# First sweep: gate products copied from PSUM by VectorE, the gate's last multiplication from the copy on GpSimd

## The chip, the core and the metric

The kernel runs on one core of a Trainium2 chip. The metric is the device time of one execution in microseconds; the median of three runs before the change was 1300.88 us (1297.87 to 1301.57). The engines are TensorE (PE in the profile; PEld is its loading of weights), VectorE (DVE), ScalarE (ACT), GpSimd (POOL) and SyncE (SP, which here only issues DMAs). Each engine works through its own queue in order, and waits on semaphores for the others.

## The reference

One layer of an encoder over 2048 positions of width 1024. A combined projection `x @ w_in` feeds two groups of heads. Group A is a gated linear attention with a forward and a backward scan in chunks; its output is normalised per head and multiplied with a SiLU gate. Group B is a latent attention with a dense softmax, gated in the same way. Both halves go through one output projection, and a layer norm of `alpha * x + mixer(x)` ends the layer. The change concerns group A's gate alone:

```python
    o = rms_norm(o_fwd + o_bwd, norm_g)
    o = o.reshape(B, S, D_GLA).astype(gate.dtype)
    return o * jax.nn.silu(gate)
```

## The kernel before

All products are made in float32 from a high and a low part of each operand, three matmuls for one product (`mm3`, L417 to L421). A high part is a rounding copy on ACT (`hi`, L362 to L367), a low part the subtraction of the high part from the original, on DVE or POOL (`lo`, L369 to L371). L365 and L371 therefore stand for many different operations in the profile, which are told apart by the tiles they write.

The kernel has four stages: a first sweep over 16 chunks of 128 positions, from chunk 15 down to chunk 0 (`sweep_a`), the late gates and the weights of the next stage (`late_gates`), a second sweep over the chunks upwards (`sweep_c`), and the softmax attention with the output projection (`attention`, `OutProj`).

For a chunk the first sweep makes three groups of products (`ipa`, 288, 384 and 384 columns), then the 512 columns of the gate (`ipg`, `gate_products`). These four results take turns in the two PSUM banks of the pool `ip`: the second group of the next chunk comes into the bank in which the gate's products lay. Between them stand the operations of the chunk before: transposes of q and k (`qT`, `kT`, L937 and L961), the decayed `qd` (L941) and `kd` (L965), their splitting (`qbh`, `qbl`, `kh`, `kl`), the transposed keys (`kt`, L979), the products `Ap`, `Up` and `Op`. The gate's decay comes from the low-rank part `lr` of the first group: `lr` is split on ACT and DVE (`ga_lr`), transposed by PE (`lrT`, L869), copied by ACT (`lrTs`), and multiplied by PE into `z` (L881). From `z` come, over three ACT steps and DVE's `za` (L891), the scans L902 and L904, and from those `E` (L914) and its two exponentials (L918, L920), which `qd` and `kd` need. `cw` (L927) are the decays of the state.

POOL makes the low part of the next but one chunk's input (`xal`, L371; on DVE for the first chunks), and the update of the running state (`Us` L1042, `Sb` L1048 and L1067, `Sm` L1063).

The gate itself is `silu` (L1485 to L1496): three ACT steps, an exponential, a logarithm and an exponential, make the sigmoid in an SBUF tile `gs` or `ub`; DVE then multiplies it with the products, which it reads from PSUM. Fourteen gates, those of chunks 13 to 0, run in the sweep (`ga_gs`, L839, in the first steps; `gate_end`, L829, in the others and for chunk 0) with tag `gs`; those of chunks 15 and 14 come behind it, with tag `ub`. Each result is stored to `u_s` (L833 or L846), and the second sweep reads it (`c_lu`). The stores of chunks 0 and 1 are issued by POOL, all others by SP.

In the first steps (chunks 14 to 12) the order of the work on every engine is written out by hand (`ORDER_A`). From chunk 11 on a scheduler sets it, from the program's order, the places in `STEPS_A` and its own estimate of when each operation is ready. It also puts operations of different engines that use the same PSUM bank one behind the other. The second sweep starts with chunk 0; its loads from `oi_s`, `qd_s` and `su_s` (L1381) stand in SP's queue with the loads of small weights (L1153). Its POOL operations `Sf` (L1399, L1402) and `SU` (L1407) make the state from `su_s`, which is split into `MMb`, and PE multiplies it into `Ob` (L1430, L1431).

Of the kernel before, what the change touches and what calls it, by code (L numbers as in the profile page):

```python
# [9 lines left out]
F32 = mybir.dt.float32  # L10
# [3 lines left out]
ALU = mybir.AluOpType  # L14
# [340 lines left out]
class K:  # L355
# [1129 lines left out]
    def silu(self, pool, g, shape, tag, name):  # L1485

        nc = self.nc
        t = self.sl = pool.tile(shape, F32, tag=tag, name=f"{tag}{name}", bufs=3 if tag == "ub" else 1)
        nc.scalar.activation(t, g, AF.Exp, scale=-1.0)
        yield 0  # L1490
        nc.scalar.activation(t, t, AF.Ln, bias=1.0)
        yield 1
        nc.scalar.activation(t, t, AF.Exp, scale=-1.0)
        yield 2
        nc.vector.tensor_tensor(t, g, t, ALU.mult)
        yield 3  # L1496


# [525 lines left out]
```

## Time and profile before

| | |
|---|---|
| median of 3 runs | 1300.88 us (1297.87 to 1301.57) |
| profiled execution | 1303.84 us, its span 1301.6 us |
| granted TensorE clock over the span | 0.996 |
| first sweep, repeating part, 95 to 342 us | 247 us; DMA share 0.25 |
| late gates and start of the second sweep, 342 to 366 us | 24 us; PE busy 22.98, DMA share 0.90 |
| second sweep, 366 to 640 us | 274 us; PE busy 269.60, POOL 157.80 |
| attention, 640 to 1245 us | 605 us; PE busy 598.61 |
| end, 1245 to 1302 us | 57 us; PE busy 48.43 |

A row of the profile's groups names the line, the engine, the operation, the tile written and those read, the shape and the count; behind the bar stand the busy time in us and the mean time of one in ns, and then the time for which the engine stood idle before them and what ended it. A row of the timeline has the start in us, the duration, and the instruction (xN: that many in a row), with an idle time of the engine before it in brackets. A row of the waits names who waited for whom, the total in us, how often, and the longest.

### The profile page before, as it was taken

How to read it: one execution, taken by the hardware profiler on the slowest of the kernel's cores; microseconds unless marked ns; L12 is line 12 of the kernel's file. 1: busy time of each engine (PE TensorE's matmuls, PEld its weight loads, DVE VectorE, ACT ScalarE, POOL GpSimd, SP SyncE). 2: the span in 40 equal slices, each digit the busy share in tenths (PEclk: the TensorE clock that was granted, in tenths of full speed). 3: DMA queues.
4: the chain of work that ended last, by engine and by line, in shares of the span. 5: the costliest groups of instructions: out<-in, count | busy, mean ns of one | idle time of the engine just before them, and what ended most of it. 6: DMA issues, size and time to landing. Idle time of an engine off the chain costs nothing.

```text
span 1301.6 us, 19963 instructions
## 1 busy us (share of the span) xinstructions
PE 1273.0 (98%) x7017; PEld 1122.8 (86%) x7017; DVE 927.6 (71%) x1712; ACT 817.4 (63%) x1387; POOL 785.4 (60%) x500
## 2 busy tenths in 40 slices
PE   7999999999999999999999999999999999998997
PEld 7999999999889999999788888888888888886886
DVE  6865664545665555555888888888888888386998
ACT  7765556565676566555788887888888887411110
POOL 0244232332567666661398888889999999934441
PEclk9999999999999999999999999999999999999999
DMA  8232222131566555656301112212233110376563
GB/s 288 72 90 66 81 66 81 53 94 53 200 203 192 187 179 200 206 179 203 96 1 41 42 41 50 52 46 57 57 89 90 41 41 25 121 241 163 189 203 102
DMA packets 113964, 145.82 MB, mean 112 GB/s; under 512 B 18018, under 2 KB 70630, under 8 KB 113864
## 3 DMA queue, kind: packets, MB, share of 16 engines
q1 hardware_dynamic: 105176, 142.41, 35.6%
q0 software_dynamic: 768, 2.10, 0.4%
q8 instruction: 56, 0.92, 0.3%
q10 hardware_dynamic: 7920, 0.03, 0.3%
q14 instruction: 44, 0.36, 0.1%
HBM read 94.14 MB, written 50.36 MB: 111 GB/s over the span
## 4 chain that ended last, share of the span: by engine, by line
PE 83%; DMA 4%; DVE 3%; ACT 3%; POOL 2%; issue 2%; SPq 0%; DVEq 0%; POOLq 0%; ACTq 0%
PE o L419 4%; PE o L420 4%; PE pS L1533 4%; PE o L421 4%; PE pS L1535 4%; PE pS L1536 4%; PE pS L1537 4%; PE pS L1534 4%; PE ipa L419 4%; PE ipa L421 3%; PE ipa L420 3%; PE pz L420 2%; PE pz L419 2%; PE pz L421 2%; PE ipg L419 2%; PE ipg L420 2%
## 5 line engine op out<-in xcount | busy, mean ns | idle before, releaser
L371 POOL TENSOR_TENSOR pl<-s,ph 128x1024 fp32r<-128x1024 f32 x128 | 306.4, 2413 | 58.4 <-ACT ph L365 54.6
L1555 DVE TENSOR_TENSOR rm<-pS,rm 128x512 f32<-128x512 f32 x210 | 144.9, 690 | 36.6 <-ACT s L1542 31.5
L1542 ACT ACTIVATE s<-pS 128x1024 f32<-128x1024 f32 x128 | 131.5, 1027 | 60.8 <-PE pS L1537 52.3
L1579 DVE TENSOR_TENSOR s<-s,mb 128x1024 f32<-128x1024 f32 x128 | 151.2, 1213 | 9.1 <-PE mb L1573 9.0
L1042 POOL TENSOR_TENSOR Us<-Us,cw 128x512 f32<-128x512 f32 x16 | 18.6, 1162 | 212.4 <-DVE Us L1040 180.7
L365 ACT ACTIVATE ph<-s 128x1024 fp32r<-128x1024 f32 x128 | 135.1, 1057 | 17.1 <-PE o L421 16.6
L1583 ACT ACTIVATE s<-s 128x1024 f32<-128x1024 f32 x128 | 131.4, 1050 | 13.4 <-DVE s L1579 13.3
L419 PE MATMUL ipa<-wah,xah 128*128 128x384 f32 (+1 forms) x384 | 131.2, 342 | 6.9 <-ACT wah L365 6.4
L420 PE MATMUL ipa<-wal,xah 128*128 128x384 f32 (+1 forms) x384 | 125.5, 327 | 0.1
L421 PE MATMUL ipa<-wah,xal 128*128 128x384 f32 (+1 forms) x384 | 124.8, 325 | 0.0
L1533 PE MATMUL pS<-qh,ckvT_h 128*128 128x512 f32 x256 | 102.5, 400 | 0.8 <-ACT s L1583 0.4
L419 PE MATMUL o<-ph,vh 128*128 128x512 f32 x256 | 101.0, 395 | 0.0
L421 PE MATMUL o<-ph,vl 128*128 128x512 f32 x256 | 99.8, 390 | 0.0
L1536 PE MATMUL pS<-rh,krs 128*128 128x512 f32 x256 | 99.8, 390 | 0.0
L1535 PE MATMUL pS<-qh,ckvT_l 128*128 128x512 f32 x256 | 99.8, 390 | 0.0
L1537 PE MATMUL pS<-rl,krs 128*128 128x512 f32 x256 | 99.7, 389 | 0.0
L1534 PE MATMUL pS<-ql,ckvT_h 128*128 128x512 f32 x256 | 99.7, 389 | 0.0
L420 PE MATMUL o<-pl,vh 128*128 128x512 f32 x256 | 99.7, 389 | 0.0
L371 POOL TENSOR_TENSOR ol<-of,oh 128x512 fp32r<-128x512 f32 x32 | 42.9, 1343 | 70.4 <-ACT oh L365 69.6
L1606 DVE TENSOR_TENSOR ap<-ap,s 128x512 f32<-128x512 f32 x120 | 83.1, 692 | 2.6 <-ACT s L1583 0.7
L419 PEld LDWEIGHTS ipa<-wah,xah 128*128 128x128 f32 x384 | 72.9, 190 | 9.9 <-ACT wah L365 6.6
L419 PE MATMUL pz<-xch,wzh 128*128 128x256 f32 x256 | 74.8, 292 | 0.0
(325 smaller groups left out, 3825.2 us busy)
## 6 DMA issues: line engine op xcount, KB each, us to landing
xcf<-xT_dram SPq DMA_DIRECT2D x16, 512.0 KB, 4.5
xr<-x_dram SPq DMA_DIRECT2D x16, 512.0 KB, 5.7
out_dram<-rr SPq DMA_DIRECT2D x32, 256.0 KB, 2.4
xaf<-xT_dram SPq DMA_DIRECT2D x14, 512.0 KB, 3.8
oib<-oi_s SPq DMA_DIRECT2D x16, 256.0 KB, 3.9
qdb<-qd_s SPq DMA_DIRECT2D x16, 256.0 KB, 5.0
SU<-su_s SPq DMA_DIRECT2D x16, 256.0 KB, 4.4
ub<-u_s SPq DMA_DIRECT2D x16, 256.0 KB, 4.2
```

What stands on the lines that cost most here:

```text
L365: return nc.scalar.activation(dst, src, AF.Copy).ins
L371: return e.tensor_tensor(dst, src, hi.bitcast(F32), ALU.subtract).ins
L419: mm(out, ah, bh, start=start, stop=False)
L420: mm(out, ah, bl, start=False, stop=False)
L421: mm(out, al, bh, start=False, stop=stop)
L1533: mm(ps[:, e], kh, qh, start=True, stop=False)
L1534: mm(ps[:, e], kh, ql, start=False, stop=False)
L1535: mm(ps[:, e], kl, qh, start=False, stop=False)
L1536: mm(ps[:, e], kr, rh, start=False, stop=False)
L1537: mm(ps[:, e], kr, rl, start=False, stop=True)
L1555: V.tensor_tensor(d["rm"], src[:, e], d["rm"], ALU.max)
L1579: V.tensor_tensor(s, s, d["mb"][:, None, :].to_broadcast([P, 2, QB]), ALU.subtract)
```

## The change

In the first sweep's gates (tag `gs`) DVE now copies the gate's products from PSUM into a new SBUF tile `gc`, behind the first ACT step, and the last multiplication reads that copy, on POOL instead of DVE. The late gates (tag `ub`) are as before. Nothing else is edited; but the scheduler and the written order place the copy where the first ACT step is placed, and the multiplication keeps its place among POOL's operations as it had it among DVE's.

```diff
         t = self.sl = pool.tile(shape, F32, tag=tag, name=f"{tag}{name}", bufs=3 if tag == "ub" else 1)
         nc.scalar.activation(t, g, AF.Exp, scale=-1.0)
+        mult = nc.vector
+        if tag == "gs":
+            gc = pool.tile(shape, F32, tag="gc", name=f"gc{name}", bufs=1)
+            nc.vector.tensor_copy(gc, g)
+            g, mult = gc, nc.gpsimd
         yield 0
         nc.scalar.activation(t, t, AF.Ln, bias=1.0)
         yield 1
         nc.scalar.activation(t, t, AF.Exp, scale=-1.0)
         yield 2
-        nc.vector.tensor_tensor(t, g, t, ALU.mult)
+        mult.tensor_tensor(t, g, t, ALU.mult)
         yield 3
```

In the order of instructions that the changed program is built to, POOL has the multiplication behind `xal` and ahead of `Us` in each repeating step; for chunk 13 it stands ahead of `Sm`, and for chunk 0 ahead of `Us`, whose store now comes behind the gate's. DVE has the copy between `oi` and `qd`, `kd` directly behind `qd`; for chunk 13 the copy stands ahead of the scans, for chunk 12 ahead of `E` (L914). ACT has `kh` ahead of `lr`, PE has `lrT` one product earlier in ten steps, and SP has the store to `u_s` ahead of the four stores of `qd`.

## The prediction

> **What bounds the kernel now.** I read the page's busy times first, then the busy times by stage.
>
> ```profile
> span 1301.6 us, 19963 instructions
> PE 1273.0 (98%) x7017; PEld 1122.8 (86%) x7017; DVE 927.6 (71%) x1712; ACT 817.4 (63%) x1387; POOL 785.4 (60%) x500
> ```
> ```profile
> 95.00:342.00 247.00, 246.79 (x1530) 231.09 (x1529) 134.15 (x286) 146.91 (x316) 80.98 (x61) 1.00 0.25 71
> ```
>
> The last row is the stage of the change, the repeating part of the first sweep (columns: stretch, its length, then busy time of PE, PEld, DVE, ACT, POOL): PE is busy for 246.79 of 247 us, DVE for 134, POOL for 81. So only what makes PE wait, or wait less, moves the end. The waits of PE's weight loads, asked for 58 to 95 us and then for 95 to 342 us, say how much the change can win:
>
> ```profile
> PEld ipa L419 <- DVE gs L1495: 0.7, 1, 0.7
> ```
> ```profile
> PEld ipa L419 <- DVE gs L1495: 2.0, 11, 0.2
> ```
>
> Twelve times the next chunk's second product group waits until the gate's last multiplication has read the PSUM bank: 2.7 us in all. That is the most that an earlier release can give.
>
> **The change part by part.** Fourteen gates lose a VectorE multiplication out of PSUM, and get a copy there and a multiplication on GpSimd. Prices, by group:
>
> ```profile
> L1495 DVE TENSOR_TENSOR gs<-ipg,gs 128x512 f32<-128x512 f32 x14 | 9.6, 682 | 0.8 <-ACT gs L1493 0.8
> ...
> L566 DVE TENSOR_SCALAR sin<-sin 128x512 f32<-128x512 f32 x3 | 1.3, 422 | 0.0
> ...
> L1627 DVE COPY acc<-ap 128x512 f32<-128x512 f32 x1 | 0.7, 673 | 0.0
> ```
> ```profile
> L1872 POOL TENSOR_TENSOR of<-of,gr 128x512 f32<-128x512 f32 x32 | 41.7, 1302 | 6.0 <-DMA of<-ob_s 4.7
> ```
>
> The copy costs 0.67 us, as much as the multiplication that it replaces (0.68): DVE wins no time. POOL gets 14 x 1.30 us, and it has room. What counts is where they fall. One step of the repeating part:
>
> ```profile
> 285.45 0.69 DVE L941 SCALAR_TENSOR_TENSOR qd<-qT,E 128x512 f32<-128x512 f32 x1 [3.67 <-PE qT L937]
> 286.06 0.68 DVE L1495 TENSOR_TENSOR gs<-ipg,gs 128x512 f32<-128x512 f32 x1
> 286.65 0.68 DVE L965 TENSOR_TENSOR kd<-kT,E 128x512 f32<-128x512 f32 x1
> 287.25 1.39 DVE L371 TENSOR_TENSOR qbl<-qd,qbh 64x512 fp32r<-64x512 f32 x2
> 288.67 0.69 DVE L371 TENSOR_TENSOR kl<-kd,kh 128x512 fp32r<-128x512 f32 x1
> 289.28 0.18 DVE L371 TENSOR_TENSOR lr<-ipa,lr 128x32 fp32r<-128x32 f32 x1
> ```
> ```profile
> 283.99 0.58 ACT L1489 ACTIVATE gs<-ipg 128x512 f32<-128x512 f32 x1
> ...
> 285.26 0.63 ACT L1493 ACTIVATE gs<-gs 128x512 f32<-128x512 f32 x1
> 286.17 1.28 ACT L365 ACTIVATE qbh<-qd 64x512 fp32r<-64x512 f32 x2 [0.28 <-DVE qd L941]
> ...
> 289.50 0.38 ACT L365 ACTIVATE q<-ipa 128x256 f32<-128x256 f32 x1 [1.08 <-DVE lr L371]
> ...
> 290.26 0.28 ACT L365 ACTIVATE lrTs<-lrT 98x128 fp32r<-98x128 f32 x1
> ```
> ```profile
> 284.22 2.41 POOL L371 TENSOR_TENSOR xal<-xaf,xah 128x1024 fp32r<-128x1024 f32 x1 [1.26 <-DMA su_s<-Sm]
> 300.41 1.04 POOL L1042 TENSOR_TENSOR Us<-Us,cw 128x512 f32<-128x512 f32 x1 [13.79 <-DVE Us L1040]
> ```
> ```profile
> 286.79 0.44 PE L419 MATMUL ipa<-wah,xah 128*128 128x384 f32 x1
> ...
> 289.36 0.42 PE L419 MATMUL ipa<-wah,xah 128*128 128x384 f32 x1
> 289.62 0.28 PE L869 MATMUL lrT<-ident,lr 128*98 128x128 f32 x1
> ...
> 290.62 0.64 PE L881 MATMUL z<-lrTs,wg 98*128 98x128 f32 x4
> ```
>
> The copy waits for the gate's first exponential (both read the bank, and the program puts them one behind the other): 284.6 to 285.3, in the 3.67 us in which DVE waits for qT. Cost nothing; if that cover were gone, qd would start later by as much. The bank is free at 285.3, the product at 286.79 no longer waits. kd moves up to 286.06.
>
> The multiplication stands behind xal on POOL. The third exponential ended at 285.9, so it starts when xal ends, at 286.6, and takes 1.29 to 1.30 us: to 287.9 or 288.0. Behind it POOL idles until 300; the result's store, now ahead of the four qd stores on SP's queue, has no reader before the second sweep. So far no cost. But DVE then wants qbl, both of whose inputs lie in SBUF. The trace of before has this meeting once, in an earlier chunk:
>
> ```profile
> 88.39 1.04 POOL L1067 TENSOR_TENSOR Sb<-Sb,cw 64x512 f32<-64x512 f32 x1
> ```
> ```profile
> 88.50 2.20 DVE L371 TENSOR_TENSOR qbl<-qd,qbh 64x512 fp32r<-64x512 f32 x2
> ```
>
> The pair took 2.20 us instead of 1.39. POOL had begun 0.11 us earlier and ended at 89.43; the first qbl of the pair ended 0.54 us behind that. Operations with a PSUM input, as qd and gs above beside xal, keep their 0.69. So whoever starts first holds the other back. Here the first qbl is ready when the first half of qbh is done, at 286.8: POOL leads by about 0.2 us. First qbl to 288.41 or 288.54, the second 0.73 later (the rest of the 2.20), kl 0.03 behind it, lr 0.61 behind the start of kl (288.67 to 289.28): lr ends at 289.95 to 290.08 instead of 289.46.
>
> PE now comes to lrT earlier: the new order puts it ahead of the product that stood at 289.36, 2.57 us behind the one at 286.79 (which itself comes 0.1 sooner): 289.27. It waits there until 0.05 behind lr's end (as the product at 286.79 came 0.05 behind the end of gs, 286.74): 290.00 to 290.13. z came 1.16 us behind lr's end (289.46 to 290.62), over ACT's q, kth and lrTs, and comes no sooner than that now: 291.11 to 291.24, a little more since PE has one product more between lrT and z. z, and all that PE does behind it, moves by **+0.49 to +0.68 us a step**; I take 0.6. Ten steps have this form (chunks 10 to 0 but the one in which ACT loads the sine table): **+6.0**. The ends for the unknown hold: -0.1 a step if no subtraction is held back (only the bank's wait goes), and 0.14 more than 0.6 if the first qbl runs its full 0.68 behind POOL's end rather than 0.54.
>
> The Trainium skill (SBUF — State Buffer, "Who interferes with whom") says that a DVE instruction with two SBUF inputs and a GpSimd instruction that reads SBUF share a port pair, and that the second fully blocks until the first finishes. The row agrees on who waits, but a full block would add the 0.14 per step named above, and give +7.4 for the ten.
>
> Chunk 13's gate (the first) puts the copy ahead of DVE's scans, about 2.3 us later, and the multiplication against them on POOL; the work behind has room: Al would end at about 66.0, and PE needs it then. Cost 0, at most 0.5.
>
> ```profile
> 63.74 0.89 DVE L371 TENSOR_TENSOR Al<-At,Ah 128x512 fp32r<-128x512 f32 x1
> ```
> ```profile
> 66.01 0.28 PE L1016 MATMUL Op<-VV,Ah 128*128 128x256 f32 x1
> ```
>
> Chunk 12's gate is worse, since its copy stands ahead of the subtraction into E:
>
> ```profile
> 81.51 0.68 DVE L914 TENSOR_TENSOR E<-E,cl 128x512 f32<-128x512 f32 x1
> ```
> ```profile
> 82.96 0.58 ACT L1489 ACTIVATE gs<-ipg 128x512 f32<-128x512 f32 x1
> ```
> ```profile
> 83.19 2.39 POOL L371 TENSOR_TENSOR xal<-xaf,xah 128x1024 fp32r<-128x1024 f32 x1 [3.16 <-PE Op L1017]
> ```
> ```profile
> 89.90 0.27 PE L869 MATMUL lrT<-ident,lr 128*98 128x128 f32 x1
> ```
>
> The copy waits for the exponential (83.54) and ends at 84.2; E (SBUF inputs) then meets xal, and ends at 86.1 instead of 82.2. Behind E come, in ACT's new order and one behind the other, two exponentials, oi, the gate's third step, four cw and kh (about 0.6 each, the cw 0.85 together, by the like rows above: an estimate of 3.8 us), then kl and lr on DVE (0.8): lr is there for lrT at about 90.75 instead of 89.90, or at 91.65 if POOL's next multiplication, which starts at the same time, holds kl back too. **+0.85 to +1.75**, taken as 1.3; the 0.7 us of bank wait is inside it.
>
> At the end of the sweep POOL multiplies chunk 0's gate (from 356.4, when the third exponential ends) ahead of Us, and stores the gate ahead of su_s:
>
> ```profile
> 355.70 0.63 ACT L1493 ACTIVATE gs<-gs 128x512 f32<-128x512 f32 x1
> ```
> ```profile
> 356.21 1.04 POOL L1042 TENSOR_TENSOR Us<-Us,cw 128x512 f32<-128x512 f32 x1 [3.56 <-DVE Us L1040]
> 357.54 0.57 POOL L1043 DMA_DIRECT2D su_s<-Us  x1 [0.30 <-POOL Us L1042]
> ...
> 371.83 1.80 POOL L1402 TENSOR_TENSOR Sf<-Sf,SU 64x512 f32<-64x512 f32 x1 [6.03 <-DMA SU<-su_s]
> ```
> ```profile
> SPq L1153 <- DMA su_s<-Us: 1.8, 1, 1.8
> ```
> ```profile
> 378.81 0.38 PE L1430 MATMUL Ob<-MMb,qhb 128*128 128x256 f32 x1 [0.23 <-POOL MMb L371]
> ```
>
> Us shifts by 1.5 us, su_s by 1.8 and the oi store behind it by 1.2. SP's loads wait for both landings in turn, so the load of SU, behind them, shifts by 1.1 to 1.8; POOL runs without a gap from SU to MMb, for which PE waits already. **+1.1**, between 0 (if the queue catches up) and 1.8.
>
> Sum: 6.0 + 1.3 + 1.1, less 0.2 for the one step whose bank wait simply goes: **+8.2 us**, with bounds +5.5 and +10.5. The profiled execution took 1303.84 us (its span and 2.2 around it), so 1312.0 there; it lies 2.96 above the median of 1300.88, which would become **1309.1**.
>
> **The rivals.** (1) *Not slower: DVE keeps the way to SBUF.* If qbl starts ahead of POOL's multiplication, and qbl, qbl and kl follow so closely that POOL gets no gap, the multiplication falls into POOL's 13.79 us and costs nothing. What stays is the bank's gain (the 0.7, and twelve less one times the 0.1 by which products came late: 1.7; at most 2.7) and the end of the sweep: -2.7 to +1.1, likeliest -1.7 + 1.1 = -0.6, 1300.3. It decides at the 0.2 us by which POOL leads. For: POOL begins only when xal ends. Against: xal's end is tied to PE as qbl is, so the lead is the same in each step; and should POOL get a gap between the subtractions, it holds back the next one, with about the same loss. (2) *Slower still: the copy is held back too.* If the copy uses both ways, it waits for xal (286.6) and qd comes at 287.2, 1.75 late: about 18 us over ten steps, 1319. Against: the copy out of PSUM took 673 ns where a one-input operation inside SBUF took 422, so it runs at single rate; and qd and gs, out of PSUM, ran beside xal unhindered.
>
> The skill (VectorE: DVE Perf Modes, "Why PSUM operands drop a tier") says that a PSUM operand excludes the mode that needs both ports; the 673 agrees.
>
> **How the numbers follow.** Forecast case 0.76, rival 1 0.17, rival 2 0.07. About 0.3% (3.9 us) is what a measurement of this kernel can tell from no change. Rival 1 gives 0.03 faster (its low end and scatter of the runs) and 0.14 within; of the forecast case 0.03 may fall short of 3.9 us; the rest is slower: 0.80. The range goes from 1302 (the forecast case with seam and chunk 12 free and a shorter hold, and the upper end of rival 1) to 1313 (all upper bounds and the scatter); it leaves out most of rival 1 and rival 2, under 0.2.
>
> **What would show it.** In the changed profile: the first qbl of a repeating step lasting some 1.6 us beside POOL's gs; PE's wait for lr before lrT, 0.7 to 0.9 us ten times, in place of the wait for gs; each repeating step longer by 0.6 us; E near 84 lasting nearly 2 us; SU's load at 367. The prediction is wrong if qbl keeps 0.69 us, or if POOL's gs begins behind qbl and kl; if PE's wait is absorbed further down the step; or if the copy lasts over 0.8 us.

## The result, and the profile after

The changed kernel takes 1310.24 us (median of 6 runs, 1308.22 to 1312.43) against 1301.09 (6 runs, 1297.87 to 1303.66): a ratio of 1.0071, 95% interval 1.0059 to 1.0084, or +9.2 us (7.7 to 10.9). The forecast was 1309.1, in a range of 1302 to 1313.

The profiled execution took 1308.22 us. The top of its page, and the busy times of the repeating part of the first sweep (stretch, length, then PE, PEld, DVE, ACT, POOL):

```profile
span 1306.4 us, 19976 instructions
PE 1271.0 (97%) x7017; PEld 1121.9 (86%) x7017; DVE 944.9 (72%) x1712; ACT 815.9 (62%) x1387; POOL 803.3 (61%) x514
```
```profile
95.00:342.00 247.00, 240.55 (x1496) 226.28 (x1495) 142.01 (x276) 143.19 (x309) 93.85 (x71) 1.00 0.24 70
```

PE, busy for 246.79 of these 247 us before, now stands still for 6.4. DVE is busy for 7.9 us longer with ten instructions fewer: some of them take longer than before. The waits of PE's weight loads, in 58 to 95 us and in 95 to 345 us:

```profile
PEld lrT L869 <- DVE lr L371: 2.6, 1, 2.6
```
```profile
PEld lrT L869 <- DVE lr L371: 8.7, 10, 0.9
```

The twelve waits for `gs` are gone, and ten waits for `lr` of up to 0.9 us have come, with one of 2.6 us in the steps ordered by hand. The step that the prediction worked through, 7 us later here: DVE, POOL and PE.

```profile
291.63 0.69 DVE L1493 COPY gc<-ipg 128x512 f32<-128x512 f32 x1 [2.83 <-ACT gs L1489]
...
293.09 0.68 DVE L965 TENSOR_TENSOR kd<-kT,E 128x512 f32<-128x512 f32 x1
293.87 2.30 DVE L371 TENSOR_TENSOR qbl<-qd,qbh 64x512 fp32r<-64x512 f32 x2
296.20 0.69 DVE L371 TENSOR_TENSOR kl<-kd,kh 128x512 fp32r<-128x512 f32 x1
296.81 0.18 DVE L371 TENSOR_TENSOR lr<-ipa,lr 128x32 fp32r<-128x32 f32 x1
```
```profile
291.25 2.40 POOL L371 TENSOR_TENSOR xal<-xaf,xah 128x1024 fp32r<-128x1024 f32 x1 [1.26 <-DMA su_s<-Sm]
293.62 1.29 POOL L1500 TENSOR_TENSOR gs<-gc,gs 128x512 f32<-128x512 f32 x1
```
```profile
295.83 0.60 PE L979 MATMUL kt<-ident,kd 128*128 128x128 f32 x4
297.05 0.32 PE L869 MATMUL lrT<-ident,lr 128*98 128x128 f32 x1 [0.63 <-DVE lr L371]
```

POOL begins 0.25 us ahead of `qbl`. The pair of subtractions takes 2.30 us instead of 1.39, `lr` ends at 296.99, and PE waits until 297.05. The copy beside `xal` keeps its 0.69.

How much later each part of the sweep is, is read from a small operation that every chunk has once, ACT's copy of `lrT`: the view of the tile gives its duration (ns: shortest, median, longest) and its first and last start, here before and after.

```profile
L365 ACT ACTIVATE lrTs<-lrT x16: 262/282/291, 21.3 to 334.4; 98x128 fp32r<-98x128 f32 x16
```
```profile
L365 ACT ACTIVATE lrTs<-lrT x16: 258/280/288, 21.5 to 343.0; 98x128 fp32r<-98x128 f32 x16
```

From first to last these are 313.1 and 321.5 us: **the sweep is 8.4 us longer**. I call this the sweep's length below, since one profile measures it more finely than the runs measure the whole. Behind the sweep little is added: the second sweep's first `Ob` stood at 378.81 and stands 8.5 later, the last product of the attention (`o`) 9.2 later. The last `o` before, then both after:

```profile
L421 PE MATMUL o<-ph,vl x256: 388/389/398, 643.5 to 1142.5; 128*128 128x512 f32 x128
```
```profile
L1430 PE MATMUL Ob<-MMb,qhb x64: 278/333/386, 387.3 to 592.6; 128*128 128x256 f32 x64
...
L421 PE MATMUL o<-ph,vl x256: 388/389/398, 652.3 to 1151.7; 128*128 128x512 f32 x128
```

The spans differ by 4.8 only: from the last `o` to the end, where no line of the change works, the execution of before took 159.1 us and this one 154.7. In the profiles of all kernels here that end takes between 153.8 and 159.1 us, so spans are not compared below.

### The profile page after: what moved, and what is told of

Same layout as the page of the kernel before. It is cut to its first block, busy times and chain, and to the rows that moved or that the text cites. A ratio compares the mean times of both kernels' runs of the same rounds, so it can differ in the third digit from the quotient of the medians.

```text
span 1306.4 us, 19976 instructions
## 1 busy us (share of the span) xinstructions
PE 1271.0 (97%) x7017; PEld 1121.9 (86%) x7017; DVE 944.9 (72%) x1712; ACT 815.9 (62%) x1387; POOL 803.3 (61%) x514
## 4 chain that ended last, share of the span: by engine, by line
PE 54%; DVE 6%; DMA 5%; POOL 2%; ACT 2%; issue 1%; SPq 1%; DVEq 0%; ACTq 0%; POOLq 0%
PE o L419 4%; PE pS L1538 4%; PE o L420 4%; PE pS L1539 4%; PE o L421 4%; PE pS L1541 4%; PE pS L1540 4%; PE pS L1542 4%; DMA xr<-x_dram 2%; PE pz L420 2%; PE pz L421 2%; PE pz L419 2%; PE ipm L421 1%; PE ipm L419 1%; PE ipm L420 1%
```

## The experiments

Each kernel was timed beside the kernel before; experiment 4 has a single run. “Longer” is said against the sweep of 313.1 us, and the code shows the lines that matter, with “...” where lines are left out.

**1. Chunks 11 to 1 alone.**

```diff
-        if tag == "gs":
+        if tag == "gs" and 1 <= int(name) <= 11:
```

> The change in the gates of chunks 11 to 1 alone; chunks 13, 12 and 0 as before. Theory (GpSimd's multiplication, which starts first, holds back VectorE's subtractions from SBUF): each of ten steps is later by about 0.52 us, the sine step by 0, the hand-ordered steps by 0: +5.2, about 1306.5 us, TensorE waiting ten times for lr ahead of lrT. Rival (the loss lies in the hand-ordered steps and in the seam to the second sweep, the steady steps lose nothing): 1301.

Measured: 1306.25 against 1301.95, ratio 1.0037 (1.0025 to 1.0049). Tile view:

```profile
L365 ACT ACTIVATE lrTs<-lrT x16: 260/279/288, 22.1 to 340.5; 98x128 fp32r<-98x128 f32 x16
```

The sweep is 318.4 us long, +5.3, with ten waits for `lr` as in the change. The steady steps are more than half of the loss; the hand-ordered steps and the seam have to account for the rest.

**2. The copy without GpSimd.** The multiplication reads the copy, on VectorE.

```diff
-            g, mult = gc, nc.gpsimd
+            g = gc
```

> The copy stays, the multiplication from the copy goes back to VectorE, in all fourteen gates. Theory: now VectorE's own multiplication has two SBUF inputs and meets xal on GpSimd, which started earlier; it ends 0.54 us behind xal's end instead of taking 0.68, kd, qbl, kl and lr come 0.44 later, ten steps of about +0.42, and chunk 12's E meets xal as in the change: +5 to +7, 1306 to 1308. Rival (what costs is the multiplication on GpSimd, through its queue or its length): without it the early release of the bank remains and the time is 1299 to 1302.

Measured: 1308.20 against 1301.95, ratio 1.0048 (1.0034 to 1.0062). Tile view, and one step on DVE and POOL:

```profile
L365 ACT ACTIVATE lrTs<-lrT x16: 259/280/289, 21.4 to 340.4; 98x128 fp32r<-98x128 f32 x16
```
```profile
290.71 1.11 DVE L1500 TENSOR_TENSOR gs<-gc,gs 128x512 f32<-128x512 f32 x1
```
```profile
288.87 2.40 POOL L371 TENSOR_TENSOR xal<-xaf,xah 128x1024 fp32r<-128x1024 f32 x1 [1.26 <-DMA su_s<-Sm]
```

No multiplication of the gate is on POOL, and the sweep is 5.9 us longer all the same: 0.4 in each of the ten like steps, 1.6 in the steps ordered by hand. The multiplication, 0.68 us out of PSUM beside the same `xal`, takes 1.11 out of SBUF, and ends 0.55 behind `xal` (291.82 and 291.27). So a loss of this size needs no added work on POOL: a meeting of two operations that read SBUF is enough.

**3. The meeting without the change.** The kernel before, with a product on POOL that nobody reads, behind the subtraction into `xal` (`low`).

```diff
+        low = self.lo(xl[:, :, 0], xf, xh[:, :, 0], "dve" if i < 4 else "pool")
+        if i > 5:
+            with self.after(low):
...
+                    nc.gpsimd.tensor_tensor(self.spare, self.rm_t, self.rm_t, ALU.mult)
```

> The kernel before, its gates untouched, with one more multiplication of 128x512 on GpSimd of a constant tile into a spare one, directly behind xal in ten steps (one of them is the sine step); no other engine's order changes and nobody reads the result. Theory: qbl meets it, lr comes about 0.5 later, nine steps of +0.4 to +0.5: +4, about 1305. Rival (order of the instructions, or the copy in VectorE's queue, makes the wait): 1301, no wait for lr.

Measured: 1304.94 against 1301.95, ratio 1.0025 (1.0012 to 1.0038). Tile views, and one step on DVE and POOL:

```profile
L365 ACT ACTIVATE lrTs<-lrT x16: 260/280/288, 22.6 to 337.6; 98x128 fp32r<-98x128 f32 x16
```
```profile
290.02 1.63 DVE L371 TENSOR_TENSOR qbl<-qd,qbh 64x512 fp32r<-64x512 f32 x2
```
```profile
289.35 1.04 POOL L815 TENSOR_TENSOR spare<-rmask 128x512 f32<-128x512 f32 x1
```

The sweep is 1.9 us longer, half of what I expected (the runs, +1.6 to +4.9 us, allow both): a tile times itself takes POOL 1.04 us, not the 1.30 of two tiles. The subtraction, which wanted to start at 290.02, was held up until 290.39, and the pair took 0.24 more than 1.39: nine steps of 0.22 are 2.0. So the size follows the overlap, and the mechanism holds with every other instruction in its old place.

**4. Two of them** (a single run): the same, twice in a row.

> The kernel before with two multiplications of the constant tile behind xal in ten steps, in place of one (1.04 us each). Theory in the form of the prediction (the two engines take turns where GpSimd gets a gap): the first qbl waits for the first multiplication, the second multiplication for the first qbl, the second qbl for the second multiplication: qbl, qbl over some 2.4 us instead of 1.63, lr 0.8 later than with one, steps of +1.0. Rival (VectorE, once it has the way, keeps it through qbl, qbl, kl): lr as with one, +0.22 a step, the second multiplication ending behind kl.

Measured: 1309.02 us, where 22 runs of the kernel before have a median of 1301.33. Tile views of `lrTs` and of the spare tile, and one step on DVE and POOL:

```profile
L365 ACT ACTIVATE lrTs<-lrT x16: 263/280/289, 21.8 to 343.6; 98x128 fp32r<-98x128 f32 x16
```
```profile
L815 POOL TENSOR_TENSOR spare<-rmask x20: 1033/1050/1372, 109.5 to 318.0; 128x512 f32<-128x512 f32 x20
```
```profile
294.46 2.37 DVE L371 TENSOR_TENSOR qbl<-qd,qbh 64x512 fp32r<-64x512 f32 x2
```
```profile
293.78 2.49 POOL L815 TENSOR_TENSOR spare<-rmask 128x512 f32<-128x512 f32 x2
```

The sweep is 8.7 us longer, 0.97 for each of nine steps. POOL's second multiplication took up to 1.37 us, since it waited for the first `qbl`; the second `qbl` then waited for it and ended at 296.83, 0.56 behind POOL's 296.27. The engines take turns, instruction by instruction. DVE does not keep the way through `qbl`, `qbl` and `kl`, on which the prediction's first rival rested.

**5. The copies of chunks 13 and 12 later**, with the gate's third step, so that `E` no longer stands behind them.

```diff
-            nc.vector.tensor_copy(gc, g)
...
+            late = int(name) >= 12
+            if not late:
+                nc.vector.tensor_copy(gc, g)
...
+            if late:
+                nc.vector.tensor_copy(gc, g)
...
         nc.scalar.activation(t, t, AF.Exp, scale=-1.0)
```

> The change, but the copies of chunks 13 and 12 are issued with the gate's third step on ScalarE, so behind E on VectorE and no longer ahead of the scans and of E. Theory: E is no longer held up, the losses of chunk 13 (1.34 by lrTs) and of chunk 12 (1.45) go, down to 0 to 0.3 each, the ten steady steps stay at 0.52: about 1307.4. Rival (in those steps it is GpSimd's multiplication and its queue, not the copy's place): 1310.

Measured: 1308.09 against 1301.95, ratio 1.0046 (1.0030 to 1.0062).

```profile
L365 ACT ACTIVATE lrTs<-lrT x16: 258/278/288, 23.1 to 341.4; 98x128 fp32r<-98x128 f32 x16
```

The sweep is 318.3 us long, as in experiment 1 where these chunks were left alone: with the copy moved, and with it POOL's multiplication, which waits for the copy, the whole loss of both chunks is gone, 3.2 us of the change's 8.4. Which of the two had cost it is not told apart here.

**6. Chunk 13 alone** (`int(name) == 13`).

> The change in chunk 13's gate alone. The prediction's step: 0 to 0.5, since the work behind the scans has room. Theory after the trace of the changed kernel: the copy puts the scans back by 2.46 and GpSimd's multiplication and Sm hold back two tiny instructions behind them (a copy of 2 elements, a subtraction of 4) by 1.8 more, Al is 1.5 late for Op, and lr too: +1.4 to +1.7, 1302.7 to 1303. Of this the copy alone is worth 0.2 to 0.5, as the run with the multiplication on VectorE shows.

Measured: 1301.67 against 1300.53, ratio 1.0005 (0.9996 to 1.0014), which does not tell 0 from 1.4. The profile does: tile view, waits (57 to 95 us), DVE and POOL.

```profile
L365 ACT ACTIVATE lrTs<-lrT x16: 257/280/288, 21.5 to 336.0; 98x128 fp32r<-98x128 f32 x16
```
```profile
PEld Op L1017 <- DVE Al L371: 0.9, 1, 0.9
...
PEld Op L1016 <- ACT Ah L365: 0.4, 1, 0.4
```
```profile
61.65 1.19 DVE L908 COPY cl<-E 128x2 f32<-128x2 f32 x1
...
63.08 0.89 DVE L912 TENSOR_TENSOR cl<-cl 128x4 f32<-128x4 f32 x1
...
66.54 0.98 DVE L371 TENSOR_TENSOR Al<-At,Ah 128x512 fp32r<-128x512 f32 x1
```
```profile
61.29 1.52 POOL L1500 TENSOR_TENSOR gs<-gc,gs 128x512 f32<-128x512 f32 x1 [13.28 <-ACT gs L1498]
62.89 1.05 POOL L1063 TENSOR_TENSOR Sm<-Sb,cw 64x512 f32<-64x512 f32 x1
```

The sweep is 1.4 us longer. A copy of two elements in each partition, 0.15 us elsewhere, ends with POOL's multiplication (62.84 and 62.81), and a subtraction of four with `Sm` (63.97 and 63.94). With the copy's wait they bring `Al` to 67.52, and PE waits 0.4 and 0.9 us for its two parts.

**7. Chunk 0 alone** (`int(name) == 0`).

> The change in chunk 0's gate alone. The prediction's step: the store of su_s<-Us lands 1.8 us later, SP's queue waits for it, SU and the first Ob come 1.1 later: 1302.4. Rival, as the trace of the changed kernel looks: the wait for su_s gets longer by 1.9, but the next one, for oi_s, goes, and SU is loaded as soon after the sweep as before: 0 to 0.4, 1301.3 to 1301.7.

Measured: 1303.00 against 1300.53, ratio 1.0024 (1.0014 to 1.0033).

```profile
L365 ACT ACTIVATE lrTs<-lrT x16: 260/280/287, 23.0 to 336.1; 98x128 fp32r<-98x128 f32 x16
...
L1430 PE MATMUL Ob<-MMb,qhb x64: 278/333/384, 381.6 to 586.6; 128*128 128x256 f32 x64
```

The sweep has its 313.1 us. From the last `lrTs` to the first `Ob` are 45.5 us, 1.1 more than the 44.4 of before: the prediction's figure. In the profile of the change itself the stretch is 44.3. Across the other profiles it lies between 43.9 and 46.6, so a shift of 1 us is not settled by one profile of each. The runs say +1.8 to +4.3; what makes them exceed 1.1 stays open.

**8. GpSimd's multiplication later.** Chunks 11 to 1 as in experiment 1, but ACT's third step stands behind the high parts of the next step's `lr`, so that the multiplication starts behind the subtractions. The gate stops after its second step; `gate_rest`, called with the second high part of that `lr`, does the rest and the store.

```diff
+        if 1 <= c <= 11:
+            next(gen), next(gen)
+            self.rest = gen, self.sl, c
+            return
...
+    def gate_rest(self, lr):
...
+        with self.after(lr):
+            next(gen)
+        for _ in gen:
+            pass
+        self.store(c).dma_start(self.u_s[c], sl)
```

> As the run with chunks 11 to 1 alone changed, but ScalarE makes the gate's third step behind the high parts of lr in the next step, so that GpSimd's multiplication starts 2.4 us later, behind the subtractions qbl and kl. Same copy, same multiplication on GpSimd, same order on TensorE. Theory: nothing is held back, lr is there 0.4 us before TensorE comes to lrT, and only the gain of the early bank remains: -0.1 a step, 1300 us. Rival (what costs is lrT one product earlier on TensorE, or GpSimd's work as such): +5, 1306.

Measured: **1297.46** against 1301.33, ratio 0.9973 (0.9963 to 0.9982), faster than before the change. Tile view, and one step on DVE and POOL (the lines of this file stand 16 lower):

```profile
L365 ACT ACTIVATE lrTs<-lrT x16: 255/271/309, 22.1 to 331.6; 98x128 fp32r<-98x128 f32 x16
```
```profile
284.92 1.41 DVE L371 TENSOR_TENSOR qbl<-qd,qbh 64x512 fp32r<-64x512 f32 x2
```
```profile
286.96 1.28 POOL L1516 TENSOR_TENSOR gs<-gc,gs 128x512 f32<-128x512 f32 x1 [2.26 <-ACT gs L1514]
```

The same copy and the same multiplication on the same engine, put 2.3 us later (4.66 behind the start of `xal` instead of 2.38), turn +5.3 into -3.6: about 0.30 in each of ten steps, and 0.6 in the step with the sine table. In the ten, PE's order is that of experiment 1; in the sine step it is not (`lrT` stands earlier among the products `Ap`, the first `Up` later), so its 0.6 is not the bank's alone.

**9. TensorE comes to lrT later.** Experiment 1 with `lrT` and `z` one product of three matmuls later. In the trace `lrT` then stands three matmuls later than in the change, and two later than in the kernel before.

```diff
-STEPS_A = {(0, 4): [("q", "prev"), ("k", "prev")], (1, 3): [("kt", "prev"), ("lrT", "cur")],
-           (1, 5): [("z", "cur"), ("cw", "cur")], (1, 7): [("intra", "prev")], (2, 3): [("state", "prev")],
+STEPS_A = {(0, 4): [("q", "prev"), ("k", "prev")], (1, 3): [("kt", "prev")], (1, 4): [("lrT", "cur")],
+           (1, 6): [("z", "cur"), ("cw", "cur")], (1, 7): [("intra", "prev")], (2, 3): [("state", "prev")],
```

> As the run with chunks 11 to 1 alone changed, but lrT and z stand one product later on TensorE. Theory: the first qbl still takes some 1.6 us and lr is as late as in the change, but TensorE comes to lrT 0.53 us later and waits 0 to 0.1: steps as long as before, 1301 (1300 to 1302). Rival (the late lr holds the step at another place, z or Ap, so that the loss only moves): +3 to +5.

Measured: 1300.74 against 1301.33, ratio 0.9997 (0.9988 to 1.0005). Tile view and waits (95 to 345 us):

```profile
L365 ACT ACTIVATE lrTs<-lrT x16: 260/279/288, 21.6 to 335.2; 98x128 fp32r<-98x128 f32 x16
```
```profile
PEld lrT L869 <- DVE lr L371: 4.3, 10, 0.4
```

`qbl` and `lr` are as late as in the change, and the loss is gone, the sweep +0.5. The waits, larger than I expected, just use up what the bank gives. So the order on PE decides how much a late `lr` costs: from `kt` to the first `Ap` a step takes 0.3 us more here than in experiment 8, and 0.8 more in the change.

**10. Chunk 12's bank as well.** Experiment 8, with a copy in chunk 12 too and its multiplication left on VectorE. In the order written by hand the gate's first step stands one place later, so that the copy comes behind `E`.

```diff
+        if tag == "gs" and 1 <= int(name) <= 12:
...
+            g, mult = gc, nc.vector if int(name) == 12 else nc.gpsimd
```

> The run with the third step made late, and in chunk 12 a copy in VectorE's idle time behind E with the multiplication from the copy left on VectorE at its old place: the bank is free 2.9 us sooner there. Theory: TensorE's wait of 0.7 goes as well: 0.5 to 0.7 faster than the run without it, 1299.4, if VectorE's multiplication from SBUF meets nothing on GpSimd (xal ended 0.9 before, Sm starts 0.07 behind its end). Otherwise that multiplication or the one behind it is held and the 0.7 is lost again.

Measured: 1296.57 against 1301.33, ratio 0.9967 (0.9955 to 0.9980): not distinguishable from experiment 8. Tile view and waits (58 to 95 us):

```profile
L365 ACT ACTIVATE lrTs<-lrT x16: 260/271/309, 21.0 to 330.3; 98x128 fp32r<-98x128 f32 x16
```
```profile
PEld z L897 <- ACT lrTs L365: 0.6, 1, 0.6
```

The wait of 0.7 for `gs` went, and PE waited 0.6 for `lrTs` in its place: the sweep is 0.2 shorter, not 0.7. In that step the bank had hidden another limit.

## Why the prediction was right, and where its terms were off

**The steady steps (forecast 0.6 each, +6.0; measured +5.2).** The mechanism was right in every link: POOL's lead (0.2 forecast, 0.25 measured), the end of the first `qbl`, `lr` 0.5 late, PE's wait before `lrT`. Experiment 2 makes the meeting without the new POOL work, 3 without the change, 4 doubles it, 8 takes it away, 9 leaves it and takes away most of the cost. The sizes are read from PE's starts in one step of each profile, in us behind the step's first `qT`; the other like steps agree within 0.1.

| | second group of `ipa` | `kt` | `lrT` | `z` | first `Ap` | next step's `qT` |
|---|---|---|---|---|---|---|
| before | 1.76 | 3.98 | 4.59 | 5.59 | 7.16 | 22.09 |
| the change | 1.66 | 3.77 | 4.99 | 6.20 | 7.69 | 22.62 |
| experiment 8 | 1.66 | 3.76 | 4.20 | 5.38 | 6.88 | 21.79 |
| experiment 9 | 1.65 | 3.76 | 4.99 | 6.20 | 7.18 | 22.08 |

The early bank brings `kt` forward by 0.21, where I had put 0.1: the row of 0.2 in the waits was nearer than the 0.1 by which one product was late. From `kt` to `z` the late `lr` costs 0.82 (2.43 us against 1.61 before and 1.62 in experiment 8), where the forecast had 0.7. So `z` is 0.61 later, as forecast, but by luck: both terms were 0.1 too small, and they have opposite signs. “All that PE does behind it” does not follow by the same 0.6: from `z` to the first `Ap` are 1.57 us before and 1.49 in the change and in experiment 8. In the steps read, these 0.08 go with how long `lrTs` is there before `z`: where `z` starts 0.08 behind the end of `lrTs` (before, experiments 2 to 4), the next matmul comes 0.47 behind `z`, and where it starts 0.19 or more behind (the change, experiments 1, 8 and 9), 0.40. Of the 0.30 that experiment 8 gains in a step, then, 0.2 are the bank's.

**The size of the hold.** The prediction had to choose between 0.54 behind POOL's end and a full subtraction, 0.68. In the step shown POOL ended at 294.91 and the first `qbl` of the pair at 295.45: 0.54. The Trainium skill (SBUF — State Buffer, "Who interferes with whom") lets the second instruction block until the first is finished; by this trace some 0.14 of a 0.68 us instruction goes on beside it (an estimate, 0.68 less 0.54). Its sentence that the issue order decides who blocks agrees with experiment 4, where POOL's second multiplication waited for the first `qbl`, and the second `qbl` for that multiplication.

**Chunk 12 (forecast +1.3, within 0.85 to 1.75; measured about +1.75).** ACT's fourth and fifth `lrTs`, which come behind the gates of chunks 13 and 12, before and after:

```profile
69.41 0.26 ACT L365 ACTIVATE lrTs<-lrT 98x128 fp32r<-98x128 f32 x1
...
90.59 0.27 ACT L365 ACTIVATE lrTs<-lrT 98x128 fp32r<-98x128 f32 x1
```
```profile
71.30 0.26 ACT L365 ACTIVATE lrTs<-lrT 98x128 fp32r<-98x128 f32 x1
...
93.93 0.28 ACT L365 ACTIVATE lrTs<-lrT 98x128 fp32r<-98x128 f32 x1
```

They are 1.89 and 3.34 later, 0.2 of it since the start. Experiment 6 puts a lasting 1.35 on chunk 13, so about 1.75 is chunk 12's, the upper end: `E` took 1.95 us beside `xal`, and `kl`, ahead of `lr` on DVE, took 1.57 us: it met `Sm` (91.46 to 92.50), which had moved behind the multiplication.

```profile
85.75 1.95 DVE L914 TENSOR_TENSOR E<-E,cl 128x512 f32<-128x512 f32 x1
...
91.47 1.57 DVE L371 TENSOR_TENSOR kl<-kd,kh 128x512 fp32r<-128x512 f32 x1 [0.64 <-ACT kh L365]
```

**Chunk 13 (forecast 0, at most 0.5; measured +1.35): the step that failed.** "The work behind has room: Al would end at about 66.0, and PE needs it then" did not count that small instructions between the scans and `E` are held too, the first of them a copy with one input, and that each is held until POOL's instruction has ended. In experiment 6 `Al` ended 1.5 later than that. Experiment 2, where the copy stood ahead of the scans too but POOL was idle beside them, lost 0.5 by that chunk's `lrTs`: the copy's wait alone is the smaller part.

**The seam (forecast +1.1, between 0 and 1.8; measured about 0 here, +1.1 in experiment 7).** The wait for `su_s` did grow, from 1.8 to 3.7 us, but the second wait in the queue, 1.8 for `oi_s` before, is not among the waits of the change: that store had landed by then. One row of before, then the change and experiment 7:

```profile
SPq L1153 <- DMA oi_s<-oi: 1.8, 1, 1.8
```
```profile
SPq L1153 <- DMA su_s<-Us: 3.7, 1, 3.7
```
```profile
SPq L1153 <- DMA su_s<-Us: 4.2, 1, 4.2
```

The two waits together are 3.6 us before and 3.7 in the change: the lower bound that the prediction named. In experiment 7 the wait for `oi_s` is gone as well, but the two sum to 4.2 and the first `Ob` comes 1.1 later. Counted from the last `lrTs`, SP issues the load of `SU` after 31.6 us before, 31.7 in the change and 32.1 in experiment 7: 0.5 of that 1.1 lie in the queue, the rest behind it. Why the wait for `su_s` differs between the two stays open, and with the scatter of that stretch so does this term.

**The sum.** In the sweep 5.2 + 1.75 + 1.35 = 8.3, with the sine step at 0 instead of -0.2; forecast were 6.0 + 1.3 + 0 - 0.2 = 7.1, and 1.1 for the seam. (The prediction's own upper bounds, 6.8, 1.75, 1.8 and 0.5 less 0.2, make 10.65 and not 10.5; nothing hangs on it.) The total agrees more closely than the terms, which is luck: the miss at chunk 13 makes up for the seam. The last 0.6 to the end of the attention I can't assign; from the first `Ob` to the last `o` the profiles of all kernels here lie between 763.3 and 764.7 us, with 763.7 before and 764.4 in the change.

## What to carry to other kernels

Before an operation goes to GpSimd, look at which VectorE instructions with their inputs in SBUF come due while it runs: the price is paid by those, and by whoever waits for them, and not by GpSimd. The same work 2.3 us later, behind those instructions, was worth 9 us here; so place it where VectorE idles or reads PSUM, and free a PSUM bank early only if the copy that frees it does not itself stand ahead of something due. Tiny instructions count: one of 0.15 us took 1.19 here, until GpSimd's instruction had ended.

## What the hardware showed that I had not expected

- A copy of 128x2 from SBUF to SBUF took 1.19 us beside POOL's multiplication (0.15 alone), though it has one input, while copies out of PSUM kept their 0.69. The Trainium skill (SBUF — State Buffer, "Who interferes with whom") counts copies in a two-port mode among those that contend; that this one ran in such a mode no run here shows.
- POOL multiplies a tile of 128x512 with itself in 1.04 us, and two tiles in 1.29.
- A wait of PE cost more than the idle time in its row. From `kt` to the first `Ap` a step takes 3.92 us in the change and 3.12 in experiment 8, with the same order on PE: 0.80 apart, where the row before `lrT` shows 0.63. `lrT` starts 1.22 behind `kt` in the change and 0.44 in experiment 8, in the time for which the record of `kt` still runs, and the row counts from the end of that record:

```profile
299.75 0.28 PE L419 MATMUL Ap<-qbh,kh 128*128 128x256 f32 x1
```
```profile
286.87 0.60 PE L995 MATMUL kt<-ident,kd 128*128 128x128 f32 x4
...
289.99 0.28 PE L419 MATMUL Ap<-qbh,kh 128*128 128x256 f32 x1
```
